# Differential attention: a half head's q and k rows copied once, both components turned together, k's second half filled by DMAs

## The chip, the core and the metric

The kernel runs on one core of one Trainium2 chip. The metric is the device time of one execution in microseconds (us). The core's engines work side by side, each through its own instructions in order: TensorE (PE; its weight loads are shown apart as PEld), VectorE (DVE), ScalarE (ACT), GpSimd (POOL) and SyncE (SP, which only issues DMAs here). An engine waits for another one by a semaphore. TensorE writes to PSUM, whose banks hold 512 f32 values in each of 128 partitions; VectorE and ScalarE read them out ("evict" them) to SBUF.

## The reference

One layer of a hybrid decoder with three branches. The change touches branch B only, the causal differential attention: 8 heads, each with two components (c = 0, 1) of 64 channels for q and for k, and a value of 128 channels, over 1024 positions.

```python
q = rms_norm(q, q_g)            # (1, 1024, 8, 2, 64)
k = rms_norm(k, k_g)
...
s = jnp.einsum('bhcqd,bhckd->bhcqk', qblk, kt).astype(jnp.float32) * scale
s = jnp.where(kpos[None, :] <= qpos[:, None], s, -jnp.inf)
p = jax.nn.softmax(s, axis=-1)
a = p[:, :, 0] - lam * p[:, :, 1]
return jnp.einsum('bhqk,bhkv->bhqv', a.astype(vt.dtype), vt)
```

Everything is f32. TensorE multiplies in a rounded f32 format (F32R in the code), so the kernel carries each operand as two parts, a rounded value ("hi") and what is left of it ("lo"), and adds the products that matter.

## The kernel before

The kernel runs in stages: norms, the memory branch, the mLSTM branch, a stretch of gate projections, the differential attention (`branch_d`, some 620 to 1165 us of the profiled execution), the branch merge and the MLP. This text is about `branch_d` and the generator `d_gemm` inside it.

`d_gemm` projects q, k and v. It goes over 16 half heads j (8 heads of 2 halves of 512 positions). A half head has 4 tiles of 128 positions; a tile is 8 steps k = 0 to 7 of 3 matmuls (`mm`, 384 columns: 128 of q, 128 of k, 128 of v), accumulated in one PSUM bank. Two banks, mm0 and mm1, take turns. After step 7 the tile is evicted: ACT copies q and k to the tile `draw`, squares them into `dscr`, and ACT and DVE split v into `dv`.

`prep` then makes a half head's operands for the scores. Its pieces do not run at once: they are closures with a due step, taken off a list while the next half head's tiles are multiplied (L929 to L931), each after the three matmuls of its step. Its transposes go to a tile `pr` in the bank that the tile at work does not use (`other_tile`, L87). The tile after that needs this bank, so its first matmul waits until `pr` is evicted.

- `q_(c)` (due 4 and 19) turns the 4 row tiles of component c. `draw` holds each 64-channel row twice side by side, so partitions 0 to 63 and 64 to 127 of `pr` get the same 64 channels. ACT writes hi to all 128 partitions of `dq`, and DVE overwrites one half of them with lo (L866, L867).
- `s_` (due 5) multiplies the k rows in `draw` by their norms: 4 multiplications of 256 columns on DVE (L874).
- `k_(c)` (due 11 and 27) turns k likewise; ACT writes hi to `dk`, DVE lo to `dkl`, each in both partition halves (L880, L881).

A score is then two matmuls over 128 partitions, `dq` against `dk` and against `dkl`, so that hi and lo of q meet hi and lo of k.

`branch_d` goes over 64 blocks s of 128 queries (8 for each head). In one s it issues on PE: the scores of component 0 (`sc`), three steps of `d_gemm`, the values of s-2 (`po`), two steps, the scores of component 1, one step, the transposes `tp` of s-1, and two steps more. By this count a tile's steps 3, 4 and 5 follow the scores of component 0; then come `po`, steps 6 and 7, the scores of component 1, and step 0 of the next tile. On the other engines each component of s has: DVE adds the mask and takes the maximum (`sc`, L989), scales it (`dst`, L993), ACT takes the exponential (`dpe`, L997); DVE combines both components (`dpe`, L1010), multiplies the normed output of the last four blocks (`doS`, L1064), and ACT and DVE evict `po` to `doS` (L1048, L1049).

PE's order is the program's order. On ACT, DVE and SP a scheduler sets the order when the kernel is built (but for what is pinned). All DMAs named here are issued by SP.

Of the kernel before, what the change touches and what calls it, by code (L numbers as in the profile page):

```python
# [10 lines left out]
F32 = mybir.dt.float32  # L11
F32R = mybir.dt.float32r
AF = mybir.ActivationFunctionType
ALU = mybir.AluOpType
# [3 lines left out]
P = 128  # L18
# [13 lines left out]
def f32(ap):  # L32
    return ap.bitcast(F32)
# [38 lines left out]
class Layer:  # L72
# [776 lines left out]
    def d_gemm(self, pool, kv, done):  # L849

        nc = self.nc
        V = nc.vector
        late = []

        def prep(raws, rr, vh):

            qT = pool.tile([P, 2, 512], F32R, tag="dq", name=self.name("dq"))
            kd = pool.tile([P, 2, 512], F32R, tag="dk", name=self.name("dk"))
            kl = pool.tile([P, 2, 512], F32R, tag="dkl", name=self.name("dkl"))

            def q_(c):
                lo = slice(64 - c * 64, 128 - c * 64)
                pt = self.other_tile()
                for i in range(4):
                    self.transpose(pt[:, i * P : (i + 1) * P], raws[i][:, c].rearrange("p a d -> p (a d)"))
                nc.scalar.activation(qT[:, c], pt, AF.Copy, scale=self.gd)  # L866
                V.scalar_tensor_tensor(  # L867
                    out=qT[lo, c], in0=pt[lo], scalar=self.gd[lo], in1=f32(qT[lo, c]), op0=ALU.mult, op1=ALU.subtract
                )

            def s_():
                for i in range(4):
                    k_ = raws[i][:, 2:4].rearrange("p c a d -> p c (a d)")
                    self.pin(V.tensor_mul(k_, k_, rr[:, i, 2:4].unsqueeze(2).broadcast_to([P, 2, P])))  # L874

            def k_(c):
                pt = self.other_tile()
                for i in range(4):
                    self.transpose(pt[:, i * P : (i + 1) * P], raws[i][:, 2 + c].rearrange("p a d -> p (a d)"))
                nc.scalar.copy(kd[:, c], pt)  # L880
                V.tensor_sub(kl[:, c], pt, f32(kd[:, c]))  # L881
                if c == 0:
                    kv.append((qT, kd, kl, vh, rr))

            return [(4, lambda: q_(0)), (5, s_), (11, lambda: k_(0)), (19, lambda: q_(1)), (27, lambda: k_(1))]

        raw = {}

        def wload(hd, k):
            r = self.rp.tile([P, 768], F32, tag="raw", name=self.name("raw"))  # L890
            nc.sync.dma_start(r.rearrange("p (k n) -> p k n", k=2), self.a["wd"][hd][:, k : k + 2, :])
            raw[hd, k] = r[:, 0:384]
            raw[hd, k + 1] = r[:, 384:768]

        def wsplit(hd, k, w):
            t = self.wp.tile([P, 2, 384], F32R, tag="w", name=self.name("w"))
            self.split(t[:, 0], t[:, 1], raw.pop((hd, k)))
            w[k] = (t[:, 0], t[:, 1])
            if k == 1:
                wload(hd, 6)  # L900

        nw = {}
        for j in range(16):
            hd, hf = divmod(j, 2)
            if j == 0:
                wload(0, 0)
                wload(0, 2)
                wload(0, 4)
                for k in range(NK):
                    wsplit(0, k, nw)  # L910
            if hf == 0:
                w, nw = nw, {}
            rr = pool.tile([P, 4, 4], F32, tag="drr", name=self.name("drr"))
            vh, raws = [], []
            for i in range(4):
                t = hf * 4 + i
                ps = self.mm_tile(384)
                for k in range(NK):
                    s = slice(t * P, (t + 1) * P)
                    self.mm3(ps, (self.hT[:, k, 0, s], self.hT[:, k, 1, s]), w[k], k == 0, k == NK - 1)  # L920
                    if hf and hd < 7:
                        if i == 1 and k == 0:
                            wload(hd + 1, 0)
                            wload(hd + 1, 2)
                            wload(hd + 1, 4)
                        if i >= 2 and k % 2 == 1:
                            wsplit(hd + 1, i % 2 * 4 + k // 2, nw)
                    elif hf and i >= 2 and k % 2 == 1:
                        self.gate_load()  # L929
                    while late and late[0][0] <= i * NK + k:  # L930
                        late.pop(0)[1]()  # L931
                    if k < NK - 1:
                        yield True
                rw = pool.tile([P, 4, 2, 64], F32, tag="draw", name=self.name("draw"))
                nc.scalar.copy(
                    rw, ps[:, 0:256].rearrange("p (a d) -> p a d", a=4).unsqueeze(2).broadcast_to([P, 4, 2, 64])
                )
                scr = pool.tile([P, 256], F32, tag="dscr", name=self.name("dscr"))
                nc.scalar.activation(scr, ps[:, 0:256], AF.Square)
                v = pool.tile([P, 2, P], F32R, tag="dv", name=self.name("dv"))  # L940
                self.split(v[:, 0], v[:, 1], ps[:, 256:384])
                vh.append(v)
                V.tensor_reduce(rr[:, i], scr.rearrange("p (a d) -> p a d", a=4), axis=AX.X, op=ALU.add)  # L943
                raws.append(rw)
                yield True
            rl = rr.rearrange("p a b -> p (a b)")
            self.rsqrt_mean(rl, rl, 64, 16)
            late = prep(raws, rr, vh)
            assert j < 4 or done[0] >= (j // 2 - 1) * 8
        for n in range(NK * 4):  # L950
            next(self.gates)
            while late and late[0][0] <= n:
                late.pop(0)[1]()
            yield True
# [799 lines left out]
```

## Time and profile before

| what | value |
|---|---|
| time, median of 3 runs (lowest to highest) | 2238.23 us (2234.21 to 2239.06) |
| the profiled execution: span from first to last instruction | 2237.1 us |
| PE, PEld busy over the span | 2180.2 us (97%), 1875.4 us (84%) |
| DVE, ACT, POOL busy over the span | 1394.6 us (62%), 1012.0 us (45%), 534.1 us (24%) |
| moved by DMA | 247.89 MB, 111 GB/s on average |

A row of a group of instructions reads: line, engine, operation, output<-inputs, shapes, count | busy us in all, mean ns of one | idle time of the engine just before them, and who ended it. A row of the timeline reads: start, us it took, engine, line, operation, output<-inputs, count, and in brackets the engine's idle time before it. Matmuls overlap in the pipeline, so what a matmul costs is seen in the distance of two starts rather than in its own duration.

### The profile page before, as it was taken

The page shows a single profiled execution, that of the slowest core. Times are in us where ns is not written, and L with a number is a line of the kernel's source. Part 1 is how long each engine was busy: PE and PEld are TensorE (multiplying, and loading weights), DVE is VectorE, ACT ScalarE, POOL GpSimd, SP SyncE. Part 2 cuts the span into 40 slices and gives each one's busy share as a digit, 9 for nine tenths or more (in the row PEclk, how much of TensorE's full clock was granted, in tenths as well). Part 3 has the DMA queues.
Part 4 walks back from the last instruction along what each step waited for, and adds up shares of the span by engine and source line. Part 5 has one row for each costly group of instructions (what it writes and reads, how often), then busy time and mean ns, then how long its engine had stood idle before and what let it go on. Part 6 is the DMA issues. An engine that isn't in the chain of part 4 may idle for free.

```text
span 2237.1 us, 30556 instructions
## 1 busy us (share of the span) xinstructions
PE 2180.2 (97%) x11222; PEld 1875.4 (84%) x11222; DVE 1394.6 (62%) x2627; ACT 1012.0 (45%) x1994; POOL 534.1 (24%) x696
## 2 busy tenths in 40 slices
PE   7999999999999999999999999999999999899999
PEld 5778788988799999999888888887887888788887
DVE  6645456554238888888752233453588887866679
ACT  6533445443336666666643111223444444543332
POOL 2100000000001111111000002202566666565553
PEclk9999999999999999999999999999999999999999
DMA  6013222210421001110134343435525444864444
GB/s 247 20 72 114 70 65 80 67 44 29 144 69 31 26 29 39 39 36 29 54 122 141 114 139 129 151 107 182 182 99 193 155 151 155 296 202 147 147 151 168
DMA packets 113780, 247.89 MB, mean 111 GB/s; under 512 B 11065, under 2 KB 19550, under 8 KB 111582
## 3 DMA queue, kind: packets, MB, share of 16 engines
q1 hardware_dynamic: 111326, 233.36, 31.6%
q10 hardware_dynamic: 2304, 12.58, 1.4%
q8 instruction: 88, 1.44, 0.3%
q14 instruction: 62, 0.51, 0.1%
HBM read 178.76 MB, written 67.14 MB: 110 GB/s over the span
## 4 chain that ended last, share of the span: by engine, by line
PE 78%; DVE 8%; DMA 5%; ACT 4%; issue 2%; POOL 1%; SPq 0%; DVEq 0%; ACTq 0%; POOLq 0%
PE mm L91 46%; PE p L91 21%; PE sc L91 6%; PE tp L94 2%; PE po L91 2%; PE pr L94 1%; DVE w L112 1%; DVE acc L67 1%; DMA raw<-in_wd 1%; DVE u L67 1%; DVE wo L67 1%; DMA kraw<-y 1%; ACT dpe L997 1%; ACT w L111 0%; DVE c L67 0%
## 5 line engine op out<-in xcount | busy, mean ns | idle before, releaser
L91 PE MATMUL mm<-w,hT 128*128 128x384 f32 (+3 forms) x2496 | 480.7, 332 | 2.6 <-ACT w L111 1.7
L91 PE MATMUL mm<-hT,w 128*128 128x512 f32 x1920 | 464.7, 396 | 2.8 <-ACT w L111 2.6
L91 PEld LDWEIGHTS mm<-hT,w 128*128 128x128 f32 x1920 | 355.2, 189 | 76.2 <-ACT w L111 2.8
L91 PEld LDWEIGHTS mm<-w,hT 128*128 128x128 f32 x2496 | 385.8, 189 | 14.9 <-ACT w L111 2.4
L91 PE MATMUL p<-xd,wo 128*128 128x512 f32 x1344 | 309.4, 392 | 5.6 <-DVE c L67 2.2
L91 PE MATMUL p<-xo,wo 128*128 128x512 f32 x1344 | 308.2, 390 | 5.5 <-DVE st L1407 1.8
L91 PEld LDWEIGHTS p<-xd,wo 128*128 128x128 f32 x1344 | 253.4, 189 | 61.5 <-DVE c L67 3.3
L91 PEld LDWEIGHTS p<-xo,wo 128*128 128x128 f32 x1344 | 251.0, 188 | 61.3 <-DVE u L67 3.7
L91 PE MATMUL mm<-kt,w 128*128 128x512 f32 x1152 | 261.6, 389 | 0.2 <-DVE w L112 0.2
L112 DVE TENSOR_TENSOR w<-raw,w 128x256 fp32r<-128x256 f32 (+3 forms) x304 | 171.9, 589 | 141.0 <-ACT w L111 139.7
L91 PEld LDWEIGHTS mm<-kt,w 128*128 128x128 f32 x1152 | 216.1, 188 | 45.5 <-DVE w L112 0.7
L111 ACT CAST w<-raw 128x256 fp32r<-128x256 f32 (+3 forms) x304 | 154.7, 531 | 177.4 <-PE mm L91 131.6
L104 ACT CAST wo<-wraw 128x896 fp32r<-128x896 f32 x122 | 115.0, 944 | 207.6 <-PE p L91 111.5
L67 DVE TENSOR_TENSOR wo<-wraw,wo 128x896 fp32r<-128x896 f32 x122 | 145.3, 1208 | 58.2 <-ACT wo L104 58.1
L1134 POOL TENSOR_TENSOR wraw<-wraw 128x128 f32<-128x128 f32 x128 | 96.8, 757 | 239.6 <-DMA wraw<-in_wdown 118.5
L997 ACT ACTIVATE dpe<-sc,dst,drr 128x256 f32<-128x256 f32 (+7 forms) x128 | 106.7, 834 | 52.3 <-DVE dst L993 49.0
L989 DVE CUSTOM_DVE_ANT_0 sc<-sc,tmask 128x256 f32<-128x256 f32 (+7 forms) x128 | 97.1, 759 | 22.0 <-PE sc L91 22.0
L127 POOL TENSOR_SCALAR hss<-hss 128x4 f32<-128x4 f32 x8 | 3.3, 412 | 392.5 <-ACT mscr L747 272.7
L127 POOL TENSOR_SCALAR drr<-drr 128x16 f32<-128x16 f32 x16 | 3.6, 225 | 373.6 <-DVE drr L943 357.0
L1137 POOL TENSOR_TENSOR wraw<-wraw 128x128 f32<-128x128 f32 x128 | 88.5, 692 | 10.0
L1136 POOL TENSOR_TENSOR wraw<-wraw 128x128 f32<-128x128 f32 x128 | 90.7, 709 | 0.0
L104 ACT CAST xd<-xd 128x1536 fp32r<-128x1536 f32 (+2 forms) x36 | 54.9, 1528 | 69.8 <-DMA xd<-r_d 69.7
(281 smaller groups left out, 3101.0 us busy)
## 6 DMA issues: line engine op xcount, KB each, us to landing
wraw<-in_wup SPq DMA_DIRECT2D x64, 256.0 KB, 3.2
r_d<-xts SPq DMA_DIRECT2D x16, 1024.0 KB, 4.1
wraw<-in_wdown SPq DMA_DIRECT2D x64, 256.0 KB, 3.1
xd<-r_d SPq DMA_DIRECT2D x19, 768.0 KB, 7.5
xd<-r_d SPq DMA_DIRECT2D x14, 1024.0 KB, 6.6
raw<-in_wgate SPq DMA_DIRECT2D x48, 256.0 KB, 3.1
gates<-gt SPq DMA_DIRECT2D x48, 256.0 KB, 2.0
raw<-in_wd SPq DMA_DIRECT2D x32, 384.0 KB, 3.6
```

Source lines behind the costliest of these rows:

```text
L67: return self.tc.keep_in_program_order(f(*a, **k))
L91: self.pin(self.nc.tensor.matmul(out, l, r, start=start, stop=stop))
L94: self.pin(self.nc.tensor.transpose(out, x, self.ident))
L104: self.A.copy(hi, src)
L111: nc.scalar.copy(hi, src)
L112: nc.vector.tensor_sub(lo, src, f32(hi))
L127: g.tensor_scalar(r, ss, 1.0 / width, EPS, op0=ALU.mult, op1=ALU.add)
L989: V.tensor_tensor_reduce(out=sc[:, 0:n], in0=sc[:, 0:n], in1=self.tmask[:, D - n : D], scale=1.0, scalar=-3.0e38, op0=ALU.add, op1=ALU.max ...
L997: nc.scalar.activation(pe[c][:, 0:n], sc[:, 0:n], AF.Exp, bias=t8[:, 2 + c : 3 + c], scale=rr[:, i, c : c + 1], accum_out=t8[:, 4 + c : 5 ...
L1134: G.tensor_add(r[:, 4], r[:, 0], r[:, 3])
L1136: G.tensor_sub(r[:, 6], r[:, 1], r[:, 0])
L1137: G.tensor_sub(r[:, 7], r[:, 2], r[:, 5])
```

## The change

The rows of a half head are copied to `draw` once (256 columns) and no longer doubled. One set of 4 transposes turns both components of q, another both of k: partitions 0 to 63 of `pr` hold component 0, 64 to 127 component 1. Eviction then goes by component, 64 partitions at a time: ACT writes hi to the component's own partitions, DVE writes lo. For q, DVE writes lo across, to the other 64 partitions. For k, DVE writes lo to the same partitions, and a DMA of 256 KB (SP's queue) copies hi and lo of the component to the other 64 partitions. `dk` and `dkl` become one tile. `s_` multiplies 128 columns in place of 256. There are three closures in place of five: `q_` due 4, `s_` due 5, `k_` due 13.

```diff
@@ -855,34 +855,37 @@
         def prep(raws, rr, vh):
 
             qT = pool.tile([P, 2, 512], F32R, tag="dq", name=self.name("dq"))
-            kd = pool.tile([P, 2, 512], F32R, tag="dk", name=self.name("dk"))
-            kl = pool.tile([P, 2, 512], F32R, tag="dkl", name=self.name("dkl"))
-
-            def q_(c):
-                lo = slice(64 - c * 64, 128 - c * 64)
+            kk = pool.tile([P, 2, 2, 512], F32R, tag="dk", name=self.name("dk"))
+            lo, up = slice(0, 64), slice(64, 128)
+
+            def turned(j):
                 pt = self.other_tile()
                 for i in range(4):
-                    self.transpose(pt[:, i * P : (i + 1) * P], raws[i][:, c].rearrange("p a d -> p (a d)"))
-                nc.scalar.activation(qT[:, c], pt, AF.Copy, scale=self.gd)
-                V.scalar_tensor_tensor(
-                    out=qT[lo, c], in0=pt[lo], scalar=self.gd[lo], in1=f32(qT[lo, c]), op0=ALU.mult, op1=ALU.subtract
-                )
+                    self.transpose(pt[:, i * P : (i + 1) * P], raws[i][:, j * P : (j + 1) * P])
+                return pt
+
+            def q_():
+                pt = turned(0)
+                for c, a, b in ((0, lo, up), (1, up, lo)):
+                    nc.scalar.activation(qT[a, c], pt[a], AF.Copy, scale=self.gd[a])
+                    V.scalar_tensor_tensor(
+                        out=qT[b, c], in0=pt[a], scalar=self.gd[a], in1=f32(qT[a, c]), op0=ALU.mult, op1=ALU.subtract
+                    )
 
             def s_():
                 for i in range(4):
-                    k_ = raws[i][:, 2:4].rearrange("p c a d -> p c (a d)")
-                    self.pin(V.tensor_mul(k_, k_, rr[:, i, 2:4].unsqueeze(2).broadcast_to([P, 2, P])))
-
-            def k_(c):
-                pt = self.other_tile()
-                for i in range(4):
-                    self.transpose(pt[:, i * P : (i + 1) * P], raws[i][:, 2 + c].rearrange("p a d -> p (a d)"))
-                nc.scalar.copy(kd[:, c], pt)
-                V.tensor_sub(kl[:, c], pt, f32(kd[:, c]))
-                if c == 0:
-                    kv.append((qT, kd, kl, vh, rr))
-
-            return [(4, lambda: q_(0)), (5, s_), (11, lambda: k_(0)), (19, lambda: q_(1)), (27, lambda: k_(1))]
+                    k_ = raws[i][:, P : 2 * P].rearrange("p (c d) -> p c d", c=2)
+                    self.pin(V.tensor_mul(k_, k_, rr[:, i, 2:4].unsqueeze(2).broadcast_to([P, 2, 64])))
+
+            def k_():
+                pt = turned(1)
+                for c, a, b in ((0, lo, up), (1, up, lo)):
+                    nc.scalar.copy(kk[a, 0, c], pt[a])
+                    V.tensor_sub(kk[a, 1, c], pt[a], f32(kk[a, 0, c]))
+                    nc.sync.dma_start(f32(kk[b, :, c]), f32(kk[a, :, c]))
+                kv.append((qT, kk[:, 0], kk[:, 1], vh, rr))
+
+            return [(4, q_), (5, s_), (13, k_)]
 
         raw = {}
 
@@ -931,10 +934,8 @@
                         late.pop(0)[1]()
                     if k < NK - 1:
                         yield True
-                rw = pool.tile([P, 4, 2, 64], F32, tag="draw", name=self.name("draw"))
-                nc.scalar.copy(
-                    rw, ps[:, 0:256].rearrange("p (a d) -> p a d", a=4).unsqueeze(2).broadcast_to([P, 4, 2, 64])
-                )
+                rw = pool.tile([P, 256], F32, tag="draw", name=self.name("draw"))
+                nc.scalar.copy(rw, ps[:, 0:256])
                 scr = pool.tile([P, 256], F32, tag="dscr", name=self.name("dscr"))
                 nc.scalar.activation(scr, ps[:, 0:256], AF.Square)
                 v = pool.tile([P, 2, P], F32R, tag="dv", name=self.name("dv"))
```

The order of the instructions moves in three places that matter below; the rows in brackets name the semaphores of the engines that an instruction waits for.

PE, around the k transposes (`pr`) of a half head whose successor's tiles begin a head; `mm` are the steps, `sc` the scores of component 0 (first) and 1 (second), `po` the values. In the kernel before:

```order
L91 MATMUL sc_7256<-dkl_6722,dq_6720 128x384
L91 MATMUL mm_7235<-w_6996,hT 128x384 x3
L94 MATMUL pr_7265<-ident,draw_6799 128x128 [waits DVE_49,PE_49]
...
L91 MATMUL mm_7235<-w_7031,hT 128x384 x3
L91 MATMUL mm_7235<-w_7059,hT 128x384 x3
L91 MATMUL po_7278<-dv_6490,daT_7241 128x256 [waits Activation_49]
...
L91 MATMUL mm_7235<-w_7075,hT 128x384 x3
L91 MATMUL mm_7235<-w_7101,hT 128x384 x3
L91 MATMUL sc_7298<-dk_6721,dq_6720 128x384 [waits Activation_49]
L91 MATMUL sc_7298<-dkl_6722,dq_6720 128x384
L91 MATMUL mm_7304<-w_6925,hT 128x384 [waits DVE_49]
```

The same engine at the same place in the changed kernel:

```order
L91 MATMUL sc_7230<-dk_6703,dq_6702 128x384
L91 MATMUL mm_7209<-w_6976,hT 128x384 x3
L91 MATMUL mm_7209<-w_7011,hT 128x384 x3
L91 MATMUL mm_7209<-w_7039,hT 128x384 x3
L94 MATMUL pr_7245<-ident,draw_6782 128x128 [waits DVE_49,PE_49]
...
L91 MATMUL po_7256<-dv_6482,daT_7215 128x256 [waits Activation_49]
...
L91 MATMUL mm_7209<-w_7048,hT 128x384 x3
L91 MATMUL mm_7209<-w_7074,hT 128x384 x3
L91 MATMUL sc_7276<-dk_6703,dq_6702 128x384 x2
L91 MATMUL mm_7282<-w_6912,hT 128x384 [waits DVE_49,PE_49]
```

The transposes stood four steps and the values ahead of the next tile's first matmul (last row); now two steps and the values.

DVE, at the same place; `dk<-pr` and `dkl<-pr` are the subtractions that free the bank of `pr`, `ISA sc` is the masked maximum. In the kernel before:

```order
L1010 SCALAR_TENSOR_TENSOR dpe_7161<-dpe_7162,dst_7163,dpe_7161 128x256 [waits DVE_49]
L881 TENSOR_TENSOR dkl_7130<-pr_7265,dk_7129 128x512 [waits Activation_49]
L1049 SCALAR_TENSOR_TENSOR doS_7281<-po_7278,dst_7049,doS_7281 128x128 [waits Activation_49]
L989 ISA sc_7298,dst_7255<-sc_7298,tmask 128x384 [waits PE_49]
L989 ISA dst_7255 128x1
L943 TENSOR_REDUCE drr_7131<-dscr_7292 128x4 [waits Activation_49]
```

The same engine at the same place in the changed kernel:

```order
L1065 TENSOR_TENSOR doS_6872<-doS_6872,dso_7185 128x512 [waits Pool_49]
L1011 SCALAR_TENSOR_TENSOR dpe_7133<-dpe_7134,dst_7135,dpe_7133 128x256 [waits DVE_49]
L884 TENSOR_TENSOR dk_7102<-pr_7245,dk_7102 64x512 [waits Activation_49]
L1050 SCALAR_TENSOR_TENSOR doS_7259<-po_7256,dst_7029,doS_7259 128x128 [waits Activation_49]
L990 ISA sc_7276,dst_7229<-sc_7276,tmask 128x384 [waits PE_49]
L990 ISA dst_7229 128x1
L884 TENSOR_TENSOR dk_7102<-pr_7245,dk_7102 64x512 [waits Activation_49]
```

There are two subtractions now, and the maximum of the second scores stands between them.

ACT, at the same place; `dk<-pr` are the copies of hi. In the kernel before:

```order
L880 CAST dk_7129<-pr_7265 128x512 [waits PE_49]
L997 ACTIVATE dpe_7253,dst_7255<-sc_7256,dst_7255,drr_6431 128x384 [waits DVE_49,Activation_49]
L1048 ACTIVATE doS_7281<-po_7278,dst_7049 128x128 [waits PE_49]
L935 COPY draw_7290<-mm_7235 128x512 [waits PE_49]
L939 ACTIVATE dscr_7292<-mm_7235 128x256 [waits Activation_49]
```

The same engine at the same place in the changed kernel:

```order
L998 ACTIVATE dpe_7227,dst_7229<-sc_7230,dst_7229,drr_6421 128x384 [waits DVE_49,Activation_49]
L883 CAST dk_7102<-pr_7245 64x512 [waits PE_49]
L1049 ACTIVATE doS_7259<-po_7256,dst_7029 128x128 [waits PE_49]
L883 CAST dk_7102<-pr_7245 64x512 [waits DVE_49]
L938 COPY draw_7268<-mm_7209 128x256 [waits PE_49]
```

There are two copies, and the second waits for DVE: for the first subtraction, which reads the same PSUM tile. So the eviction of `pr` is a chain of four: copy, subtraction, copy, subtraction. For q it is the same chain with L870 and L871.

## The prediction

> **What bounds the kernel now.** I read the busy time by stages first, since the change lies in one stage. The columns are the stretch in us, its length, and busy us with instruction counts of PE, PEld, DVE, ACT and POOL, then PE's granted clock and the DMAs' share.
>
> ```profile
> 799.50:847.50 48.00, 47.65 (x313) 45.57 (x312) 39.24 (x105) 33.32 (x78) 5.73 (x6) 1.00 0.13 32
> 847.50:860.00 12.50, 12.09 (x81) 11.58 (x80) 10.02 (x33) 7.05 (x21) 2.90 (x3) 1.00 0.14 49
> ```
>
> These two rows are one head (60.5 us) of the differential attention. PE is busy 59.74 of them, DVE 49.26, ACT 40.37. So PE is the bound there: work taken from PE shortens the stage, and any new wait of PE lengthens it by its full length, since PE has next to no idle time to hide it. DVE has 11 us of idle time in a head, but it runs strictly in order, so a wait in the wrong place costs all that is behind it.
>
> The waits of the stage (620 to 1165 us; who waited for whom, us in all, times, longest) say the same:
>
> ```profile
> PEld pr L94 <- issue: 3.9, 6, 0.7
> PE pr L94 <- DVE dst L993: 2.0, 5, 0.4
> ```
>
> These are PE's largest waits of the stage, and they stand ahead of the transposes `pr` that the change moves: 2.0 us by the first row of PE itself, up to 3.9 by its weight loads.
>
> **What is removed.** The groups of the stage that the change touches, and the nearest rows for what it adds:
>
> ```profile
> L94 PE MATMUL pr<-ident,draw 128*128 128x128 f32 x256 | 38.5, 273 | 2.1 <-DVE dst L993 2.0
> L935 ACT COPY draw<-mm 128x512 f32<-128x512 f32 x64 | 37.4, 585 | 38.0 <-PE mm L91 37.9
> L939 ACT ACTIVATE dscr<-mm 128x256 f32<-128x256 f32 x64 | 24.9, 390 | 0.0
> L874 DVE TENSOR_TENSOR draw<-draw,drr 128x256 f32<-128x256 f32 x64 | 22.9, 420 | 0.6
> L112 DVE TENSOR_TENSOR dv<-mm,dv 128x128 fp32r<-128x128 f32 x64 | 18.1, 282 | 0.6 <-ACT dv L111 0.5
> L866 ACT ACTIVATE dq<-pr,dv 128x512 fp32r<-128x512 f32 x32 | 22.0, 686 | 28.1 <-PE pr L94 28.1
> L867 DVE SCALAR_TENSOR_TENSOR dq<-pr,dv,dq 64x512 fp32r<-64x512 f32 x32 | 24.0, 749 | 19.2 <-ACT dq L866 19.2
> L880 ACT CAST dk<-pr 128x512 fp32r<-128x512 f32 x32 | 18.7, 585 | 14.1 <-PE pr L94 14.1
> L881 DVE TENSOR_TENSOR dkl<-pr,dk 128x512 fp32r<-128x512 f32 x32 | 21.9, 684 | 2.6 <-ACT dk L880 2.6
> L989 DVE CUSTOM_DVE_ANT_0 sc<-sc,tmask 128x384 f32<-128x384 f32 x16 | 8.8, 552 | 0.7 <-PE sc L91 0.7
> ```
>
> 128 of the 256 transposes go, 32 groups of four. By busy time that is 38.5/2 = 19.2 us, but a busy row counts the tail of a pipelined matmul. The chain of waits (start, us, what) has the distance itself:
>
> ```profile
> 650.69 3.95 PE mm L91 x21
> 655.08 4.20 PE mm L91 x24
> ```
>
> 650.69 + 3.95 = 654.64, and the next piece starts at 655.08: a group of transposes takes 0.44 us of PE. 32 x 0.44 = 14.1 us, which I take; by the shortest distance in the timeline (a group at 755.73, the next matmul at 756.09, below) it is 32 x 0.36 = 11.5. With the transposes later in their tile (step 5 in place of 3), the bank they need has long been evicted, and the waits above go: 2.0 to 3.9 us, I take 3.0. The gain on PE is 17.1 us, bounds 13.5 and 23.1.
>
> Off PE the change also saves. ACT's copy to `draw` falls from 585 to some 390 ns (the 256-column row, as an estimate), 64 x 0.195 = 12.5 us; DVE's `s_` from 420 to some 282, 64 x 0.138 = 8.8 us. I cost these at nothing, since PE's work covers both engines; they shorten the chains below a little. The eviction of `pr` keeps its count: per half head two copies and two subtractions for q, two and two for k, now of 64 partitions. The row of `dq` with 64 partitions costs 749 ns, no less than `dkl` with 128, so I price 64 partitions like 128 (range below: no gain from it).
>
> **What is added: waits of PE.** The next tile's first matmul needs the bank of `pr`, and `pr` is now freed by a chain of four: copy, subtraction, copy, subtraction, because the second copy waits for the first subtraction (front part, ACT's order). For q this takes 0.69 + 0.75 + 0.69 + 0.75 = 2.88 us, for k 2 x (0.585 + 0.684) = 2.54, if nothing else stands between. I follow it through the four places where it meets the rest. First, a half head whose successor opens a head (8 of 16), in the timeline of before:
>
> ```profile
> 850.23 0.68 ACT L866 ACTIVATE dq<-pr,dv 128x512 fp32r<-128x512 f32 x1
> 850.94 0.76 DVE L867 SCALAR_TENSOR_TENSOR dq<-pr,dv,dq 64x512 fp32r<-64x512 f32 x1 [1.36 <-ACT dq L866]
> 852.62 0.69 PE L91 MATMUL mm<-w,hT 128*128 128x384 f32 x3
> 855.77 0.63 PE L94 MATMUL pr<-ident,draw 128*128 128x128 f32 x4 [0.41 <-DVE dst L993]
> 856.35 0.69 DVE L1064 TENSOR_TENSOR doS<-doS,dso 128x512 f32<-128x512 f32 x1 [0.46 <-POOL dso L128]
> 857.03 0.54 DVE L989 CUSTOM_DVE_ANT_0 sc<-sc,tmask 128x384 f32<-128x384 f32 x1
> 858.14 0.68 DVE L881 TENSOR_TENSOR dkl<-pr,dk 128x512 fp32r<-128x512 f32 x1
> 858.57 0.33 PE L91 MATMUL sc<-dk,dq 128*128 128x384 f32 x1
> 858.92 0.77 PE L91 MATMUL mm<-w,hT 128*128 128x384 f32 x3
> ```
>
> - Its q: DVE's first one ends at 851.70; the second copy adds 0.69 and the second subtraction 0.75, so the bank is free at 853.15. PE's next tile stands ready at 852.62: PE waits 0.5 us.
> - Its k: DVE reached the subtraction at 858.14. Now the `doS` multiplication (0.69) stands between the maximum and it, and DVE is some 0.2 late from q, so the first subtraction runs 859.0 to 859.7; the second copy ends at 860.3. In DVE's order the maximum of the second scores (0.55) and the eviction of `po` stand ahead of the second subtraction, which then runs about 860.4 to 861.1. PE reaches the next tile at about 858.8 (the q wait above against the wait of 0.4 to 0.7 that goes): it waits 2.3 us. At the least it waits 0.55 + 0.68 = 1.2 us, since that maximum reads the scores that PE finishes just ahead of this tile; at the most, with DVE 0.8 later, 3.1.
>
> Then a half head whose successor is a head's second half (7 of 16):
>
> ```profile
> 755.73 0.60 PE L94 MATMUL pr<-ident,draw 128*128 128x128 f32 x4
> 756.09 0.78 PE L91 MATMUL mm<-w,hT 128*128 128x384 f32 x3
> 756.96 0.99 ACT L997 ACTIVATE dpe<-sc,dst,drr 128x768 f32<-128x768 f32 x1
> 757.09 0.76 DVE L867 SCALAR_TENSOR_TENSOR dq<-pr,dv,dq 64x512 fp32r<-64x512 f32 x1 [0.25 <-ACT dq L866]
> 759.36 0.69 PE L91 MATMUL mm<-w,hT 128*128 128x384 f32 x3
> 764.56 1.10 ACT L997 ACTIVATE dpe<-sc,dst,drr 128x896 f32<-128x896 f32 x1 [0.51 <-DVE dst L993]
> 764.98 1.01 DVE L1010 SCALAR_TENSOR_TENSOR dpe<-dpe,dst,dpe 128x768 f32<-128x768 f32 x1
> 767.33 0.70 PE L91 MATMUL mm<-w,hT 128*128 128x384 f32 x3
> ```
>
> - Its q: ACT does the exponential first (ends 757.95), then the second copy (to 758.7), then DVE the second subtraction to 759.5, against 759.36: PE waits 0.2.
> - Its k: the combination (1.01) now stands ahead of the first subtraction, 765.4 to 766.1; the exponential (1.10) and one eviction stand between the two copies, so the second copy ends at 767.25 and the second subtraction at 768.0, against 767.33: 0.7. DVE comes to this place late, though, since its second q subtraction ended at 759.5 where the only one ended at 757.85; `s_` gives 0.5 of this back. I take 1.4, bounds 0 and 2.0.
>
> The first half head (1 of 16) has no scores beside it: after q come 3 steps, after k 2, of 4.20/8 = 0.525 us each. 2.88 - 1.58 = 1.3, and 2.54 - 1.05 = 1.5; with some 0.15 us each to get from engine to engine, 3.1 us.
>
> Sum of the waits: 8 x (0.5 + 2.3) + 7 x (0.2 + 1.4) + 3.1 = 22.4 + 11.2 + 3.1 = 36.7 us. Bounds: 8 x 1.2 + 3.1 = 12.7, and 8 x (0.7 + 3.1) + 7 x (0.3 + 2.0) + 3.5 = 50.
>
> **What is added: 32 DMAs** of 256 KB on SP's queue. A store of that size beside them takes:
>
> ```profile
> y<-yd SPq DMA_DIRECT2D x16, 256.0 KB, 3.4
> ```
>
> The first score that needs them is 15 us behind the transposes (762.8 to 778.2 at the half head above), 9 us behind the second subtraction, and SP's loads of the next weights (`in_wd`) start behind that. I cost them at nothing on the path; without that cover it would be 3.4 us for each of 16 half heads.
>
> **The sum**, against the profiled execution's own 2237.1: 2237.1 - 17.1 + 36.7 = 2256.7. The median is 1.1 above that execution: 2258.
>
> **The rivals.** *The clock falls in the new waits.* PE's granted clock is 1.00 in this stage. Where PE waited long elsewhere, it was not:
>
> ```profile
> PE mm L91 <- ACT w L111: 2.6, 1, 2.6
> 564.00:568.00 4.00, 3.91 (x11) 0.63 0.73 246
> PE tp L559 <- ACT g_b L540: 2.4, 1, 2.4
> 240.00:244.00 4.00, 4.00 (x19) 0.67 0.44 103
> ```
>
> Behind waits of 2.6 and 2.4 us the next 4 us had 0.63 and 0.67 of the clock, about 1.4 us lost each time. My k wait of 2.3 us is at the edge. If 8 of them do this, 8 x 1.4 = 11 us come on top: 2269. The Trainium skill ("TensorE: Matmul & The Clock Gate", Part 1) has the clock halved after an idle window of about 3.4 us; by that the waits here are too short, and the traces differ from it, since 2.4 us was enough.
>
> *Faster: only the certain waits stay.* If DVE reaches each second subtraction without a backlog, PE waits 12.7 us (the lower bound) and gains 17.1: 2238.2 + 12.7 - 17.1 = 2233.8, at best 2238.2 + 12.7 - 23.1 = 2228. It decides where the waits together fall below the gain: with 3.1 of 17.1 us spent in the first half head, under 1 us in each of the other 15. For it: DVE and ACT get 21 us of work less, and each wait of PE lets them catch up. Against it: DVE's order puts the maximum between the two subtractions.
>
> *The two cancel.* Waits of 13 to 22 us: 2234 to 2243.
>
> *The DMAs come late*, because SP is held by a second subtraction or a load: 16 x 3.4 = 54 us more. Against it the 9 us of room. 2300 and above.
>
> **Chances.** Forecast (2244 to 2264) 0.54, clock 0.18, faster 0.14, cancel 0.09, late DMAs 0.05. A measurement of this kernel tells some 0.2% (4.5 us) from no change. Faster 0.14, the same 0.09, slower 0.77. The range holds all but the best of the faster cases and the late DMAs: 2234 to 2277; the likeliest case alone 2244 to 2264.
>
> **What would show it.** Transposes `pr` x128; the two copies of a k apart by one subtraction; "PE mm" waiting for DVE's `dk` in the stage, 8 times about 2.3 us and 7 times about 1.4, and for `dq` 0.5 and 0.2; scores waiting for no DMA; the clock in the stage 1.00. Wrong would be: PE's waits for DVE below 17 us in all (faster), or a wait for the DMA of `dk`.

## The result, and the profile after

The changed kernel takes 2263.63 us (median of 4 runs, 2262.48 to 2268.26) against 2238.28 us (median of 4, 2234.21 to 2239.06): ratio 1.0122, 95% interval 1.0108 to 1.0137. It is 25 us slower.

The profiled execution is the longest of the four. Its page opens with the span and the busy time of each engine:

```profile
span 2266.3 us, 30435 instructions
PE 2180.0 (96%) x11094; PEld 1871.5 (83%) x11094; DVE 1389.4 (61%) x2627; ACT 999.5 (44%) x1994; POOL 528.2 (23%) x696
```

The groups of the stage (600 to 1210 us) that the change touches: line, engine, operation, shapes and count, then busy us, mean ns, idle time before them and who ended it.

```profile
L871 DVE SCALAR_TENSOR_TENSOR dq<-pr,dv,dq 64x512 fp32r<-64x512 f32 x32 | 24.0, 750 | 27.4 <-ACT dq L870 27.4
L938 ACT COPY draw<-mm 128x256 f32<-128x256 f32 x64 | 23.7, 370 | 24.0 <-PE mm L91 22.7
L884 DVE TENSOR_TENSOR dk<-pr,dk 64x512 fp32r<-64x512 f32 x32 | 22.0, 687 | 12.1 <-ACT dk L883 11.9
L870 ACT ACTIVATE dq<-pr,dv 64x512 fp32r<-64x512 f32 x32 | 21.8, 680 | 21.2 <-PE pr L94 14.3 <-DVE dq L871 6.8
L94 PE MATMUL pr<-ident,draw 128*128 128x128 f32 x128 | 19.2, 272 | 0.0
L883 ACT CAST dk<-pr 64x512 fp32r<-64x512 f32 x32 | 18.5, 577 | 15.6 <-PE pr L94 11.2 <-DVE dk L884 3.9
```

The work did what the diff says: 128 transposes, narrower `draw` copies, and evictions of 64 partitions that cost what 128 cost before (577 to 750 ns). What is new is in PE's waits in the same stretch (who waited for whom: us in all, times, longest). First rows of before, then the two largest of after:

```profile
PE tp L94 <- ACT yd L1070: 1.7, 5, 0.4
PE mm L91 <- DVE dq L867: 0.6, 1, 0.6
PE mm L91 <- DVE dkl L881: 0.2, 1, 0.2
```

```profile
PE mm L91 <- DVE dk L884: 22.5, 16, 2.3
PE mm L91 <- DVE dq L871: 10.5, 12, 2.8
```

Before, PE waited there 0.6 us for `dq` and 0.2 for `dkl`; now it waits 33.0 us for `dq` and `dk`, always with the first matmul of a tile. The waits of `pr` for `dst` (2.0 us before) and of `tp` for `yd` (1.7) are no longer in the list. One such place in the timeline (start, us, engine, line, what, [idle before <- releaser]), ahead of a head's first tile:

```profile
873.47 0.55 DVE L990 CUSTOM_DVE_ANT_0 sc<-sc,tmask 128x384 f32<-128x384 f32 x1
873.88 0.60 PE L94 MATMUL pr<-ident,draw 128*128 128x128 f32 x4
...
874.18 0.68 DVE L1065 TENSOR_TENSOR doS<-doS,dso 128x512 f32<-128x512 f32 x1
...
874.36 0.67 ACT L998 ACTIVATE dpe<-sc,dst,drr 128x384 f32<-128x384 f32 x1 [1.21 <-DVE dst L994]
...
875.02 0.57 ACT L883 CAST dk<-pr 64x512 fp32r<-64x512 f32 x1
...
875.62 0.68 DVE L884 TENSOR_TENSOR dk<-pr,dk 64x512 fp32r<-64x512 f32 x1 [0.36 <-ACT dk L883]
...
876.34 0.58 ACT L883 CAST dk<-pr 64x512 fp32r<-64x512 f32 x1 [0.49 <-DVE dk L884]
...
876.49 0.55 DVE L990 CUSTOM_DVE_ANT_0 sc<-sc,tmask 128x384 f32<-128x384 f32 x1
...
877.13 0.69 DVE L884 TENSOR_TENSOR dk<-pr,dk 64x512 fp32r<-64x512 f32 x1
...
877.97 0.76 PE L91 MATMUL mm<-w,hT 128*128 128x384 f32 x3 [1.87 <-DVE dk L884]
```

Copy, subtraction, copy, subtraction pass the bank to and fro, from 875.02 to 877.82; the maximum (0.55) of the second scores is what DVE does between its two; PE stands 1.87 us. In a head's second half the same chain costs less:

```profile
898.59 0.77 PE L91 MATMUL mm<-w,hT 128*128 128x384 f32 x3 [0.15 <-DVE dq L871]
...
907.55 0.76 PE L91 MATMUL mm<-w,hT 128*128 128x384 f32 x3 [0.74 <-DVE dk L884]
```

A head is the clean measure of this kernel: the stretch from one group of `pr` to the same group a head later repeats within 0.1 us over the first four heads behind the first, where the clock is full. Before (first row) and after (second), with the length, busy us of PE, PEld, DVE, ACT and POOL, then the granted clock:

```profile
734.99:795.37 60.38, 59.62 (x389) 57.06 (x389) 49.14 (x137) 40.28 (x96) 8.63 (x9) 1.00 0.12 36
```

```profile
739.12:801.32 62.20, 58.43 (x374) 55.55 (x373) 48.77 (x137) 38.37 (x96) 8.63 (x9) 1.00 0.20 52
815.00:820.00 5.00, 5.00 (x23) 4.80 (x21) 2.16 (x7) 1.80 (x5) 0.00 (x0) 0.66 0.29 59
```

A head takes 1.82 us more. The next head (801.32 to 865.04) takes 63.72: behind the k wait at 814 us the clock was 0.66 for 5 us (last row), and 1.5 us went. The 29.2 us between the two profiled executions (2266.3 - 2237.1) lie so: 2.1 ahead of the first `pr`; 9.3 from there to head 1's second half (77.7 before, 87.0 after; the first half head, a q wait of 2.8 and a clock of 0.50 behind it); 14.5 in the six heads that follow (361.7 and 376.2, two of them with the clock loss); 2.7 from there to the last `po`; 0.6 behind it.

### The profile page after: what moved, and what is told of

It reads as the page before. It is cut to its first block, busy times and chain, and to the rows that moved or that the text cites. A ratio compares the mean times of both kernels' runs of the same rounds, so it can differ in the third digit from the quotient of the medians.

```text
span 2266.3 us, 30435 instructions
## 1 busy us (share of the span) xinstructions
PE 2180.0 (96%) x11094; PEld 1871.5 (83%) x11094; DVE 1389.4 (61%) x2627; ACT 999.5 (44%) x1994; POOL 528.2 (23%) x696
## 4 chain that ended last, share of the span: by engine, by line
PE 69%; DVE 15%; ACT 6%; DMA 6%; issue 3%; POOL 1%; SPq 0%; DVEq 0%; ACTq 0%; POOLq 0%
PE mm L91 41%; PE p L91 21%; PE sc L91 4%; DVE sc L990 2%; ACT dpe L998 2%; PE tp L94 2%; DVE w L112 1%; DVE acc L67 1%; DVE daT L112 1%; DVE dk L884 1%; PE po L91 1%; DVE dq L871 1%; ACT dq L870 1%; DMA xr<-h_d 1%; DVE wo L67 1%
## 5 line engine op out<-in xcount | busy, mean ns | idle before, releaser
L91 PEld LDWEIGHTS mm<-w,hT 128*128 128x128 f32 x2496 | 391.5, 190 | 51.9 <-issue 22.1
L91 PEld LDWEIGHTS p<-xd,wo 128*128 128x128 f32 x1344 | 253.7, 189 | 62.2 <-DVE c L67 3.7
L91 PE MATMUL sc<-dk,dq 128*128 128x512 f32 (+3 forms) x384 | 91.5, 347 | 0.0
```

What stands on the lines that cost most here:

```text
L91: self.pin(self.nc.tensor.matmul(out, l, r, start=start, stop=stop))
```

## Experiments

The table has each kernel's median, its ratio to the kernel before on the same chip with the 95% interval, and the median length of the six heads behind the first in its profile. Where the clock fell in some of the six, the length without that and the longer ones are given. What lies behind the last `po` took 1082 to 1088 us from one profiled execution to the next, so a few us of a total are no sign; the head lengths are.

| kernel | us | ratio | a head |
|---|---|---|---|
| before | 2238.28 | 1 | 60.39 |
| changed | 2263.63 | 1.0122 (1.0108 to 1.0137) | 62.2, two of six 63.4 and 63.7 |
| each DMA of k twice | 2266.56 | 1.0116 (1.0095 to 1.0138) | 62.2, two of six 63.7 |
| draw copied wide | 2273.92 | 1.0149 (1.0133 to 1.0165) | 64.6 |
| both copies first | 2273.11 | 1.0150 (1.0129 to 1.0171) | 64.6 |
| k's step at 11 | 2254.24 | 1.0062 (1.0043 to 1.0082) | 60.9 |
| before, 32 groups more | 2252.25 | 1.0054 (1.0039 to 1.0069) | 61.6 |
| pr copied to SBUF | 2235.38 | 0.9975 (0.9962 to 0.9988) | 59.5 |
| the same, k at 11 | 2231.89 | 0.9961 (0.9948 to 0.9974) | 58.8 |
| evicted at 128, k at 13 | 2231.08 | 0.9948 (0.9931 to 0.9966) | 58.4 |
| evicted at 128, k at 11 | 2223.05 | 0.9919 (0.9902 to 0.9935) | 57.4 |
| the same, draw wide | 2230.16 | 0.9952 (0.9921 to 0.9983) | 58.8 |

**The step of k two earlier.**

```diff
-            return [(4, q_), (5, s_), (13, k_)]
+            return [(4, q_), (5, s_), (11, k_)]
```

> The changed kernel with k's step due two steps earlier (11 in place of 13), so that two more steps of the stream (some 0.5 us each) stand between the transposes of k and the next tile's first matmul. Theory (the added time is PE waiting for the chain copy, subtraction, copy, subtraction at pr's bank): PE's waits for dk, in the changed kernel 8 times 1.87 us, 7 times 0.75 and once 2.17, fall to 8 times 0.8, 0 and 1.1: about 14.7 us less than 2263.6, so 2249, and some us more if the clock keeps full speed behind shorter waits. Rival (the time goes to the DMAs of k or to a fuller DVE, and the waits only show it): within 4 us of 2263.6, the wait turning up at another matmul.

It took 2254.24, 9.4 us less: the theory's direction, two thirds of its size. In a head's second half the k wait is gone, as expected. Ahead of a head's first tile it fell from 1.87 to 1.40, not to 0.8 (this kernel's timeline):

```profile
743.20 0.63 PE L94 MATMUL pr<-ident,draw 128*128 128x128 f32 x4
...
744.48 0.67 ACT L998 ACTIVATE dpe<-sc,dst,drr 128x384 f32<-128x384 f32 x1 [1.21 <-DVE dst L994]
...
745.14 0.57 ACT L883 CAST dk<-pr 64x512 fp32r<-64x512 f32 x1
...
747.07 0.69 DVE L884 TENSOR_TENSOR dk<-pr,dk 64x512 fp32r<-64x512 f32 x1 [0.39 <-ACT dk L883]
...
747.91 0.77 PE L91 MATMUL mm<-w,hT 128*128 128x384 f32 x3 [1.40 <-DVE dk L884]
```

The chain itself is 745.14 to 747.76. But ACT starts on it 1.94 us behind the transposes, where it was 1.14 with the step at 13 (873.88 to 875.02), since the exponential now ends later beside them (1.28 us behind them it begins, where it was 0.48). The wait is the chain plus when ACT comes to it.

**Both copies first.** The same four instructions for q and for k, in the order copy, copy, subtraction, subtraction:

```diff
...
                 for c, a, b in ((0, lo, up), (1, up, lo)):
                     nc.scalar.copy(kk[a, 0, c], pt[a])
+                for c, a, b in ((0, lo, up), (1, up, lo)):
                     V.tensor_sub(kk[a, 1, c], pt[a], f32(kk[a, 0, c]))
...
```

> The changed kernel with both ACT copies of pr ahead of both DVE subtractions, for q and k. Theory (the engines' turns and what stands between the two subtractions in DVE's order, above all the maximum of 0.55 us, make the wait longer than the chain itself): the chain is still two copies and two subtractions long, but nothing stands between: each k wait ahead of a head 0.5 to 0.9 us shorter, each q wait there 0.2 to 0.5, in all 6 to 12 us less, 2252 to 2258. Rival (only the length of the chain counts): 2263.6 within 3 us.

Neither came: 2273.11, a k wait of 3.02 us ahead of a head's first tile (none in its second half, where q's went from 0.15 to 0.90). The place in its timeline:

```profile
871.35 0.60 PE L94 MATMUL pr<-ident,draw 128*128 128x128 f32 x4
...
871.61 0.69 DVE L1067 TENSOR_TENSOR doS<-doS,dso 128x512 f32<-128x512 f32 x1 [0.51 <-POOL dso L128]
...
872.29 0.55 DVE L992 CUSTOM_DVE_ANT_0 sc<-sc,tmask 128x384 f32<-128x384 f32 x1
...
873.19 0.67 ACT L1000 ACTIVATE dpe<-sc,dst,drr 128x384 f32<-128x384 f32 x1 [1.54 <-DVE dst L996]
...
873.85 1.16 ACT L884 CAST dk<-pr 64x512 fp32r<-64x512 f32 x2
...
875.04 1.41 DVE L886 TENSOR_TENSOR dk<-pr,dk 64x512 fp32r<-64x512 f32 x2 [1.54 <-ACT dk L884]
...
876.60 0.76 PE L91 MATMUL mm<-w,hT 128*128 128x384 f32 x3 [3.03 <-DVE dk L886]
```

The chain took 2.6 us, 0.2 less than in the changed kernel. But the `doS` multiplication, which waits for POOL, now stands ahead of the maximum in DVE's order (in the changed kernel behind it, 874.18 to 873.47), so the exponential and with it the first copy begin 2.5 us behind the transposes in place of 1.14. The edit moved a second thing, so it doesn't tell whether the turns of the engines cost anything; that stays open. It shows again that the start of the chain counts as much as its length.

**pr copied to SBUF.** One ACT copy of 128x512 frees the bank; the four pieces are made from the copy:

```diff
...
+                st = pool.tile([P, 512], F32, tag="dev", name=self.name("dev"))
+                nc.scalar.copy(st, pt)
...
-                    nc.scalar.copy(kk[a, 0, c], pt[a])
-                    V.tensor_sub(kk[a, 1, c], pt[a], f32(kk[a, 0, c]))
+                    nc.scalar.copy(kk[a, 0, c], st[a])
+                    V.tensor_sub(kk[a, 1, c], st[a], f32(kk[a, 0, c]))
```

> The changed kernel, but pr is evicted by one ACT copy of 128x512 to SBUF, and the four pieces (two copies, two subtractions) are made from there; pr's bank is free after some 0.6 to 0.7 us. Theory (the bank held through four pieces is the whole loss): PE's waits for dq and dk, 33.7 us in the changed kernel, go, with the clock lost behind them (some 8 us in the profiled execution) and the restarts; what stays is the saving of 128 transposes and the waits ahead of them: 2238.2 - 17.1 = 2221, between 2215 and 2227. Rival 1 (the saving on PE is smaller than 14 us, so that without the waits the kernel is as before): 2233 to 2242. Rival 2 (ACT's 32 more copies, some 19 us, delay the exponentials and PE waits for those): above 2242.

2235.38: 28 us less than the changed kernel and slightly faster than before, not the 2221 of the theory. The waits for DVE at the bank are gone; one wait in each head is left, for ACT:

```profile
PE mm L91 <- ACT dev L883: 9.0, 7, 1.6
PE tp L94 <- DVE doS L1052: 2.3, 8, 0.9
```

That the bank's hold was the loss is thereby shown; that ACT comes late to it is a cost of its own (rival 2 in part). The time lies in the range of rival 1, a smaller saving on PE. But a wait of 1.55 us is still in each head, and the kernels below in which it goes fall under that range.

**The same with k's step at 11.**

> The kernel with pr copied to SBUF first, and k's step due at 11 in place of 13. With 13, ACT was at an exponential when k's pr was ready, and PE waited 1.55 us in each head for its copy. Theory: two steps earlier ACT comes to the copy 1.3 us before PE needs the bank, so that wait goes and a head takes 57.8 to 58.0 us (59.5 with 13, 60.4 before): 2235.4 - 9 - some 1.5 of restarts = 2225, between 2221 and 2229. Rival (the wait moves to another matmul, or q's): 2232 to 2238.

The wait for `dev` went, as the theory said, and a smaller one took its place at another instruction, as the rival said. 2231.89 is 3 us above the theory's range and at the lower edge of the rival's (a head 58.8, not 57.9):

```profile
PE pr L94 <- DVE dv L112: 5.5, 8, 0.9
PE tp L94 <- DVE doS L1052: 2.7, 8, 0.9
```

**Each DMA of k twice.**

```diff
-                    nc.sync.dma_start(f32(kk[b, :, c]), f32(kk[a, :, c]))
+                    for _ in range(2):
+                        nc.sync.dma_start(f32(kk[b, :, c]), f32(kk[a, :, c]))
```

> The changed kernel with each of the 32 DMAs of k issued twice in a row to the same place. Theory (the DMAs lie beside other work with microseconds of room): 2263.6 within 3 us, and no score waits for a DMA. Rival (the DMAs stand on the path, or hold SP's queue): some 3 us more for each of 16 half heads, 2310, or at least 10 us more.

Ratio 1.0116 against 1.0122, and its heads are the changed kernel's to 0.02 us, with the clock lost in two of six again. The DMAs cost nothing that a head shows.

**32 groups of transposes more in the kernel before.**

```diff
-                for i in range(4):
+                for i in range(4 + 4 * c):
+                    i %= 4
```

> The kernel before, with the four transposes of q's and of k's second component done twice into the same bank: 32 more groups of four transposes on PE and nothing else. It measures the term of 14.1 us. By the distance in the chain of waits (0.44 us a group): 2238.3 + 14.1 = 2252.4, and one head (from one k group to that of the next head, 60.4 us before) 1.76 us longer. By the busy row (0.60 us a group): 2257.5, a head 2.4 us longer. By the shortest distance (0.36): 2249.8, a head 1.44 longer. In the kernel with pr copied to SBUF a head took 59.5 us with a single wait of 1.55, so some 2.5 us went from a head, waits ahead of pr included: that speaks for more than 0.44.

14 us over the 2238.28 of the first comparison, 12 over the 2240.48 of its own. The rows of before and of this kernel give the price of one group:

```profile
741.00 0.60 PE L94 MATMUL pr<-ident,draw 128*128 128x128 f32 x4
...
747.60 0.60 PE L94 MATMUL pr<-ident,draw 128*128 128x128 f32 x4
```

```profile
743.74 1.04 PE L94 MATMUL pr<-ident,draw 128*128 128x128 f32 x8
...
750.78 1.03 PE L94 MATMUL pr<-ident,draw 128*128 128x128 f32 x8
```

A row of eight is 0.44 longer than one of four, and the step to the next group goes from 6.60 to 7.04. The busy row of four (0.60) counts 0.16 that is no distance. A head grew by 1.2 us, not 1.76: of its four added groups three took 0.42 to 0.44 each, the fourth vanished in the wait of 0.35 us (`tp` for ACT's `yd`) that stood behind it and is gone here.

**Evicted at 128 partitions, halves moved by DMAs alone.** One copy and one subtraction for q, one each for k, as wide as before the change:

```diff
...
+                nc.scalar.copy(hk[:, 0], pt)
+                V.tensor_sub(hk[:, 1], pt, f32(hk[:, 0]))
-                for c, a, b in ((0, lo, up), (1, up, lo)):
-                    nc.scalar.copy(kk[a, 0, c], pt[a])
-                    V.tensor_sub(kk[a, 1, c], pt[a], f32(kk[a, 0, c]))
-                    nc.sync.dma_start(f32(kk[b, :, c]), f32(kk[a, :, c]))
+                for c, a in ((0, lo), (1, up)):
+                    for b in (lo, up):
+                        nc.sync.dma_start(f32(kk[b, :, c]), f32(hk[a]))
...
-            return [(4, q_), (5, s_), (13, k_)]
+            return [(4, q_), (5, s_), (11, k_)]
```

> The changed kernel, but pr evicted at its full 128 partitions by one ACT copy and one DVE subtraction (as before the change), into a tile in SBUF from which DMAs alone put the halves across partitions (eight a half head: four of 128 KB for q, four of 256 KB for k, with those of the lower and the upper half of k both made); k's step due at 11. Theory (what costs is how long pr's bank is held: 1.3 to 1.4 us now, 2.5 to 2.9 in the changed kernel): PE's waits for dq and dk all but go, a head takes 57.8 to 58.3 us, 2222 to 2230. Rival (four times as many DMAs come late for the scores): above 2240, with waits of PE for a DMA of dq or dk.

2223.05, ratio 0.9919 (0.9902 to 0.9935): faster than both. Its head has no wait of PE at all, and its stage next to none:

```profile
730.97:788.38 57.41, 57.41 (x374) 55.56 (x373) 45.39 (x133) 36.61 (x93) 8.60 (x9) 1.00 0.38 92
```

```profile
PE po L91 <- DVE daT L112: 1.2, 2, 1.0
PE tp L94 <- DVE doS L1055: 0.9, 1, 0.9
PE mm L91 <- DVE dev L872: 0.5, 1, 0.5
PE mm L91 <- DVE dev L887: 0.3, 1, 0.3
```

No score waits for the eight DMAs of a half head. To tell the short eviction from the step, the same with k's step at 13:

> The kernel with pr evicted at 128 partitions by one copy and one subtraction and put across partitions by DMAs, but k's step at 13, as in the changed kernel (the one with 11 took 2223.05, a head 57.4 us without any wait for pr's bank). It tells how much of that is the shorter eviction and how much the step. Theory: at 13 ACT reaches the copy only behind an exponential (in the kernel with the copy to SBUF PE waited 1.55 us there for ACT alone), and the subtraction (0.68) comes on top: one wait of 2.2 us in each head ahead of the next head's first matmul, none for q and none in a head's second half; a head 57.4 + 2.2 + 0.3 for the restart = 59.9 us, 2223 + 8 x 2.5 = 2243, and 5 to 10 us more where the clock falls behind waits of this length, as it did behind those of 2.05 and 3.02. Rival (the step makes no difference once the eviction is short): 2223 within 4 us.

2231.08, a head 58.4: one wait of 0.91 us in each, so the step is worth 1.0 us of a head, and the short eviction the other 3.8 of the 4.8 from 62.2 to 57.4. These two kernels also leave ACT and DVE half as many evictions (DVE is busy 45.4 us of a head in place of 48.8), so the 3.8 are not the hold alone. The kernel with the copy to SBUF gives ACT more work, not less (40.8 us of a head in place of 38.4), and still has 2.7 us less in a head than the changed one. The 2.2 expected was too much. It was taken from the kernel with the copy to SBUF, where the exponential in front began 2.5 us behind the transposes (737.79 to 735.29); here it begins 1.1 behind them (735.02 to 733.90).

**The narrower copies undone.** ACT's copy to `draw` and DVE's `s_` at their width of before:

```diff
...
-                rw = pool.tile([P, 256], F32, tag="draw", name=self.name("draw"))
-                nc.scalar.copy(rw, ps[:, 0:256])
+                rw = pool.tile([P, 512], F32, tag="draw", name=self.name("draw"))
+                nc.scalar.copy(rw.rearrange("p (u n) -> p u n", u=2), ps[:, 0:256].unsqueeze(1).broadcast_to([P, 2, 256]))
```

> The changed kernel, but ACT's copy to draw writes 512 columns again (the 256 twice) and DVE's multiplication s_ works on 256 columns again, as before the change; no other step uses the second half. It measures what the narrower copies are worth. Prediction (12.5 us of ACT and 8.8 us of DVE lie beside PE's work): 2263.6 within 3 us, a head without clock loss 62.2 us. Rival (they stand in the chains that PE waits for): 5 to 21 us slower.

2273.92: the rival. The waits for `dk` and `dq` hardly changed (32.0 us in all, 33.0 in the changed kernel), but the k waits ahead of a head are 2.05 in place of 1.87, and behind them the clock fell in five heads of six (first to 0.66 over 750 to 755 us), where it fell in two of six in the changed kernel. Small waits of `tp` came back too, 0.4 to 0.6 us in a head.

The same undone in the kernel without waits for the bank, with 5 buffers of `draw` in place of 7:

> The kernel with pr evicted at 128 partitions and k's step at 11 (2223.05, a head 57.4 us, no wait for pr's bank), with ACT's copy to draw and DVE's s_ at 512 and 256 columns again (draw has 5 buffers in place of 7, enough for the four tiles of a half head and one more). In the changed kernel the wider copies cost 6 to 10 us: a head went from 62.2 to 64.6, with waits for pr's bank of the same sum, 0.6 us of new waits of tp and a lower clock behind each k wait of 2.05 us (behind those of 1.87 in one head of four). Theory (most of that was the clock, which falls only behind long waits): here no wait is near 2 us, so only the small waits of the transposes return, 0.3 to 1.2 us a head: 57.7 to 58.6, 2225 to 2233. Rival 1 (they cost nothing where PE does not wait): 2223 within 3. Rival 2 (they cost PE as much as there): a head 59.8, 2240 or more.

2230.16, 7.1 us more, a head 58.76 in place of 57.41. The two ratios' intervals overlap (0.9921 to 0.9983 and 0.9902 to 0.9935), so the size rests on the head. The time is inside the theory's range, the head 0.15 us above it. The head's 1.35 us are waits of 0.77 with what PE loses at each; in its timeline they stand at

```profile
737.09 0.63 PE L94 MATMUL pr<-ident,draw 128*128 128x128 f32 x4 [0.15 <-DVE dst L1000]
...
785.23 0.66 PE L94 MATMUL tp<-ident,dpe 128*128 128x128 f32 x4 [0.46 <-DVE doS L1056]
...
786.56 0.66 PE L94 MATMUL tp<-ident,dpe 128*128 128x128 f32 x4 [0.16 <-ACT yd L1077]
```

ACT's copy to `draw` waits for PE's `mm` alone there (33.0 of the 33.5 us that ACT is idle ahead of it), so the fewer buffers don't show as a cause. So the narrower copies are worth 1.35 us of a head (7 us by the totals, some 11 by eight heads) where PE waits for nothing else, and more where they keep idle time short enough for the clock.

## Why the prediction was right, point by point

It said 2258, slower, by PE waiting for the four-piece eviction; 2263.6 was measured, by that mechanism. Where one copy to SBUF frees the bank and the four pieces stay, the kernel is 28 us faster than the changed one; where one copy and one subtraction free it and DMAs do the rest, 33 us (41 with the step at 11). That shows the cause. The total came out as near as it did by luck in part (last point).

- *A group of transposes, 0.44 us:* right (0.44 measured by itself, not the 0.60 of the busy row).
- *The gain on PE, 17.1 us:* under-sized. From 60.38 to 57.41 (evicted at 128, k at 11) a head of PE's work with its old waits shrank by 2.97 us, 24 us for eight. The groups are 1.62 of it (60.38 to 58.76, the kernel with wide copies). The other 1.35 is the narrower copies. The prediction put the waits that go at 3.0 us in all, left out those of `tp` for `yd` (1.7), and gave their end to the later step of k. With k at 11 as before, they return with the wide copies and go with the narrow ones, so it is mostly the faster ACT and DVE that end them.
- *The savings of ACT and DVE at nothing, "since PE's work covers both engines":* wrong, and the one step that failed in kind. They were idle for 11 us and more of a head and still late for PE twice in each of five heads before (0.35 us for `yd`, 0.41 for `dst`): idle time elsewhere in a head does not help where other work stands ahead in the engine's order.
- *The waits, 36.7 us:* 33.0 measured, the places right, the split not: ahead of a head's first tile q 0.9 (0.5 said) and k 1.87 (2.3); ahead of its second half q 0 to 0.38 (0.2) and k 0.75 (1.4); the first half head 1.56 and 2.17, 3.7 (3.1). The first and the last of the eight ahead of a head differ: q 2.84 and k 1.53, and k 2.27 with no wait for q. The k wait came out shorter because the prediction had DVE come late to the first subtraction, and the trace has it there 0.36 us early (the row at 875.62).
- *What a wait costs beside its length:* missing from the sum. With the waits of 3.7 us taken from 62.20, a head is still 1.1 above the 57.41 of the kernel without them, some 8 us in the stage. PE's busy time has it too: 58.43 us in a head with the waits, 57.41 without them, for the same matmuls. Row by row against the kernel evicted at 128 with k at 13, whose order on PE is the same, a wait costs 0.24 us on top. 0.16 of it is a matter of counting: idle time counts from the end of the score ahead (0.28 us long), and without a wait the next matmul starts 0.12 us behind that score's start. The other 0.08 lies in the distance to the matmul behind. Some 0.3 more stands at one group of `tp` (798.04 us), whose wait of 0.09 is too short for the list.
- *The rival on the clock:* it came in part, on top of the forecast, and the sign "the clock in the stage 1.00" did not come. In the profiled execution four stretches have a lower clock, some 8 us in all. Behind k waits of 1.40 (k at 11) and 1.1 to 1.55 (copy to SBUF) the clock stayed at 1.00 in all six heads; behind 1.87 it fell in two of six, in each of two kernels; behind 2.05 and 3.02 in five of six; each time 1.5 to 1.7 us. The length of the wait alone doesn't decide: behind the one of 2.70 us in the kernel with wide copies (at 1137.67) the clock stayed, and behind 0.87 and 1.02 us in a row in the kernel with the copy to SBUF (to 1147.22) it fell. In each execution the stretches of lower clock start on one grid of 3.41 us and have 0.50 throughout; in this stage they last 3.41 us or twice that, and the 0.66 over 5 us is made of this. Two windows of that grid in the changed kernel, each around a k wait of 1.88 us and with the window behind it (columns as in the heads above, the last two the DMAs' share and GB/s):

```profile
812.29:815.70 3.41, 1.53 (x10) 1.45 (x10) 2.46 (x8) 2.18 (x7) 0.00 (x0) 1.00 0.47 97
815.70:819.11 3.41, 3.41 (x12) 3.21 (x11) 2.16 (x7) 0.77 (x2) 0.00 (x0) 0.50 0.28 56
938.58:941.99 3.41, 1.84 (x11) 1.84 (x12) 2.42 (x10) 2.36 (x7) 0.00 (x0) 1.00 0.60 124
941.99:945.40 3.41, 3.41 (x23) 3.33 (x22) 2.07 (x7) 1.17 (x3) 0.00 (x0) 1.00 0.16 32
```

The first wait lies whole in one window, the second is shared with the window ahead. In this stage, over the twelve profiled executions, PE was busy at most 1.55 us in each of the 23 windows that a drop followed, and at least 1.58 in every other window at full clock. (In the other stages the border is less sharp.) So it is the idle time that falls into one window of the grid that counts here. The Trainium skill ("TensorE: Matmul & The Clock Gate", Part 1) has the clock halved after an idle window of about 3.4 us that runs free of the program. The traces agree with the length and with the grid. They differ in that the window need not be idle throughout: 1.86 us of idle time in it was enough.

- *DMAs at nothing:* right, with twice as many too.
- *The sum:* -24 (gain) + 33.0 (waits) + 8 (restarts) + 8 (clock) = +25, of 29.2 in the profiled execution, 2.1 of the rest ahead of the stage. The forecast of +20 was two errors of 7 and 12 us that half met, which is luck: too small a gain, and waits priced at their length alone. The median stands at the upper edge of the likeliest case (2244 to 2264).

One thing in the chain may not be needed: the second copy reads partitions 64 to 127 and the subtraction ahead reads 0 to 63, and ACT stands 0.49 us until that subtraction's end. The Trainium skill ("PSUM — Partial Sum Buffer", section "PSUM bank collisions raise a hardware error") lets two engines use one bank at the same time in different groups of 32 partitions. No run here shows them at once, as the program orders the two by the whole bank.

## What to carry to other kernels

Before an edit that cuts an evicted tile in two, add up how long the bank is held, piece by piece through both engines, from when the first engine comes to it: here 2.8 us in place of 1.3 made 33 us of waits, where 128 transposes gave 13. Let the engines evict a bank in as few and as wide instructions as they can, and let DMAs that nobody waits for move data across partitions. Price a wait of the bounding engine above its length (0.24 us more here, and 1.5 to 1.7 where it lowers the clock), and don't cost savings on the other engines at nothing because those have idle time.

## What was not expected of the hardware

- The clock fell behind single waits of 1.87 us (to 0.50 for 3.41 us, 1.5 us lost), in some heads and not in others, and in none of twelve heads with waits of 1.1 to 1.55. In this stage it fell exactly where PE was busy 1.55 us or less of one window of a 3.41 us grid.
- Four times as many DMAs (128 in place of 32 in the stage, four of 256 KB and four of 128 KB a half head) cost no time that a head shows; those of k took 4.6 us from issue to landing in place of 3.0.
- Evictions of 64 partitions take as long as those of 128: ACT 577 and 585 ns, DVE 687 and 684.
